# A pool of half-size weight tiles and more steps of weight preparation in the retention part of a hybrid RG-LRU, retention and conv-FFN block

## The chip, the core and the metric

The kernel runs on one NeuronCore of a Trainium2 chip. The engines named below are PE (TensorE, the matmuls), DVE (VectorE), ACT (ScalarE), POOL (GpSimd) and SP (SyncE, which issues the loads). The metric is the device time of one execution in microseconds (us); the time of the kernel before is the median of three runs.

## The reference

One layer over 512 tokens and 16 meta tokens (528 rows), model width 1024. Cut to what is computed:

```python
xn = rms_norm(h, norm_mix_g);  z = xn @ w_in                 # 1024 -> 10752
u_rnn, u_gate, q, k, v, g_ret, ga, gb = split(z)
o_a = rg_lru(causal_dwconv(u_rnn, ...), ...) * gelu(u_gate)  # width 1280
q, k = rotary(q), rotary(k) * RET_DK ** -0.5                 # 4 heads of 256
o = retention(q, k, v)                                       # decay-weighted, v is 4 heads of 512
o_b = head_rms(o) * silu(g_ret)
mixed = sigmoid(ga) * (o_a @ w_branch_rnn) + sigmoid(gb) * (o_b @ w_branch_ret)
h = h + mixed @ w_out
up = causal_dwconv(rms_norm(h, norm_ffn_g) @ w_up, ...);  gate, val = split(up)
h = h + (gelu(gate) * val) @ w_down
out = rms_norm(h, norm_final_g)[:, 16:]
```

## The kernel before, in words

Every float32 matrix is turned into a pair of float16 tiles, hi and lo, and each product is made of three float16 matmuls (hi·hi, hi·lo, lo·hi). A weight comes in units, listed in `units` in the order of use. `unit_load` fetches one unit (mostly 1 MB) into one of three `raw` buffers (pool `wraw`), SP's loads following one another. Its preparation is a list of steps in the queue `steps`. A step splits a part of the raw unit: ACT writes the hi half into a tile `wt` (L95), DVE the lo half (L96). A split of 1024 columns takes 1.05 us on ACT and 1.22 us on DVE, one of 512 columns 0.63 and 0.69.

A *plain* unit has two steps and fills two `wt` tiles. A *fast* unit is used in a scheme of seven products in place of eight (Strassen-like, 2 x 2 blocks). Its five steps in `fast_steps` are: B11 (a half-size form, 512 columns), then B21 and B22 together, then three sums in place on DVE (L263, L264, L265, 1.22 + 0.69 + 0.69 us), then T1 with T3, then T4 with T2. Its four forms lie in four `wt` tiles, the first of which is half empty. Pool `wsp` has ten such tiles.

What sets the order of the work: the program is emitted in the order of the code, while the tile framework orders each engine's queue by data and buffer dependences and by priority; within an engine instructions run in the order of its queue. Preparation is mixed in by `tick(n)`, which emits the next n steps, unless the units from the one in use (`current[0]`) to the step's own count more tiles than `ahead[0]` by `unit_tiles`: 4 for a fast unit, 2 for a plain one. `get(u)` emits whatever of unit u is still missing. `advance(run, ...)` takes a gate unit one product further and gives out one step. `keep` is ACT's copy of a finished product out of the PSUM bank `pa` (L928 in gates, L1022 in values), which the next product in `pa` waits for.

The stages that the change touches, with their times in the profiled execution: `values(0)` (to 250), `fast_values(1)` with scores of heads 2 and 3 (254 to 281), `retention_out(0)` and the gate of head 0 with the retention outputs of head 1 (`gated(0)`, 281 to 316), `fast_values(2)` (316 to 337), `gated(1)` (to 364), `fast_values(3)` (364 to 386), `gated(2)` (to about 413), the first mixing gates `gate_a` with the last head's gate (to about 497), and the second gates `gate_b` with their products (to 640). Then come the output projection, the up stage (to 935) and the down stage.

In a gate, DVE makes `g0` and `g1` from products and kept copies (L945, L949, L956), ACT applies the function (L961), and DVE multiplies into the retention output `or` (L1111). `head_norm` (L1087 to L1104) ends in two transposes of `rt` on DVE. `L1249` is the first part of the mixing.

## Time and profile before

| | |
|---|---|
| runs | 1054.64, 1054.85, 1055.18 us (median 1054.85) |
| the profiled execution's own time | 1054.74 us |
| its span, first to last instruction | 1053.0 us |
| mean granted TensorE clock | 0.998 |
| busy PE, DVE, ACT, POOL | 1036.3, 881.2, 590.9, 6.9 us |
| bytes moved by DMA | 111.52 MB, 106 GB/s in the mean |
| loads of `w_in`, 1 MB each | 34, landing 5.1 us after issue |
| PE idle from 220 to 639 us | 7.1 us in all |
| PE idle in the last 118 us | 6.9 us, nearly all after the last matmul |

How to read it: the profile is one execution, so times in rows are measured from its first instruction, 1.7 us of the execution's own time lying outside. Rows of the timeline give start, length, engine, line, operation and tile; the bracket at their end is the idle time of that engine just before, and the engine and line whose end released it. Matmuls overlap: a row of several is the time from the first's start to the last's end.

### The profile page before, as it was taken

Reading aid. Unit: us, or ns where it says so; the run is one execution under the profiler, and the core shown is the slowest. Engines: PE = TensorE matmul, PEld = TensorE weight load, DVE = VectorE, ACT = ScalarE, POOL = GpSimd, SP = SyncE. Lnnn points to the kernel's source line nnn. Section 1 sums busy time; section 2 is a strip of 40 time slices with the busy share of each in tenths; the row PEclk is TensorE's granted clock in tenths of the full one; section 3 lists DMA queues with packets and bytes.
Section 4 is the critical chain, followed back from the end, with each engine's and each line's share of the span. In section 5 each row is a group of like instructions: output and inputs, shape, how many; then the busy total and the mean of one; then the engine's idle time right before and its main releaser. Section 6 shows DMA issues by size and latency. Waiting matters only on the chain.

```text
span 1053.0 us, 21647 instructions
## 1 busy us (share of the span) xinstructions
PE 1036.3 (98%) x9283; PEld 873.9 (83%) x9283; DVE 881.2 (84%) x1332; ACT 590.9 (56%) x947; POOL 6.9 (1%) x20
## 2 busy tenths in 40 slices
PE   8999999999999999999999999999999999999997
PEld 6888888866888888888888885588888888888884
DVE  6997899898779999988797785489989888988965
ACT  8668934334566758766454453384555555454432
POOL 2000000000000000000000000000000000000000
PEclk9999999999999999999999999999999999999999
DMA  9241353221113123334333365032432324124312
GB/s 296 93 132 60 121 174 127 82 82 41 41 41 121 53 95 106 96 112 135 106 106 120 121 203 178 18 104 93 149 119 82 121 85 152 47 67 134 102 40 80
DMA packets 109343, 111.52 MB, mean 106 GB/s; under 512 B 5706, under 2 KB 101168, under 8 KB 109248
## 3 DMA queue, kind: packets, MB, share of 16 engines
q1 hardware_dynamic: 108672, 109.74, 32.7%
q8 instruction: 72, 1.18, 0.5%
q10 hardware_dynamic: 288, 0.27, 0.1%
q0 software_dynamic: 288, 0.14, 0.1%
q14 instruction: 23, 0.19, 0.1%
HBM read 108.04 MB, written 2.10 MB: 105 GB/s over the span
## 4 chain that ended last, share of the span: by engine, by line
PE 84%; DVE 10%; ACT 3%; issue 1%; DMA 0%; ACTq 0%; DVEq 0%
PE ps L435 36%; PE P L1637 10%; PE pa L922 9%; PE pe L922 4%; PE ps L1354 4%; PE pm L435 3%; DVE wt L96 3%; PE ps L449 3%; PE pb L922 2%; PE pa L1012 2%; PE pa L1524 2%; PE ps L1079 2%; PE pe L1012 1%; ACT wt L95 1%; DVE raw L263 1%
## 5 line engine op out<-in xcount | busy, mean ns | idle before, releaser
L435 PEld LDWEIGHTS <-wt 128*128 128x128 f16 x3840 | 372.8, 97 | 51.4
L96 DVE SCALAR_TENSOR_TENSOR wt<-raw,wt 128x1024 f16<-128x1024 f32 (+2 forms) x290 | 314.5, 1100 | 55.1 <-ACT wt L95 53.8
L95 ACT ACTIVATE wt<-raw 128x1024 f16<-128x1024 f32 (+2 forms) x290 | 271.2, 956 | 128.5 <-PE P L1637 23.1
L922 PEld LDWEIGHTS <-wt 128*128 128x128 f16 x2016 | 195.3, 97 | 32.4 <-issue 5.7
L435 PE MATMUL ps<-x2h,wt 128*128 128x258 f16 (+1 forms) x1184 | 196.2, 272 | 0.0
L435 PE MATMUL ps<-xh,wt 128*128 128x258 f16 (+4 forms) x1056 | 177.0, 274 | 0.0
L435 PE MATMUL ps<-x2l,wt 128*128 128x256 f16 (+1 forms) x592 | 160.9, 272 | 0.0
L435 PE MATMUL ps<-xl,wt 128*128 128x256 f16 (+4 forms) x528 | 140.6, 274 | 0.0
L1637 PE MATMUL P<-wt,act 128*128 128x256 f16 x792 | 88.3, 273 | 0.0
L1637 PEld LDWEIGHTS <-act 128*128 128x128 f16 x792 | 77.5, 98 | 9.0
L922 PE MATMUL pa<-xs,wt 128*128 128x258 f16 x576 | 71.3, 273 | 2.0 <-ACT kept L928 1.5
L1502 DVE SCALAR_TENSOR_TENSOR cv<-ps,vt,cv 128x512 f32<-128x512 f32 x80 | 59.5, 747 | 9.1 <-ACT cv L1500 8.5
L263 DVE TENSOR_TENSOR raw<-raw 128x1024 f32<-128x1024 f32 x45 | 54.9, 1221 | 0.7
L435 PE MATMUL pm<-oa,wt 128*128 128x256 f16 (+1 forms) x480 | 54.1, 273 | 0.0
L922 PE MATMUL pa<-ob,wt 128*128 128x257 f16 x384 | 45.7, 274 | 0.6 <-ACT last L928 0.5
L1354 PE MATMUL ps<-wt,mx 128*128 128x512 f16 x192 | 44.3, 378 | 0.0
L1500 ACT ACTIVATE cv<-ps,vt,vt 128x512 f32<-128x512 f32 x40 | 30.6, 766 | 11.9 <-PE ps L435 11.9
L1524 PEld LDWEIGHTS <-wt 128*128 128x128 f16 x336 | 32.6, 97 | 4.4
L1354 PEld LDWEIGHTS <-mx 128*128 128x128 f16 x192 | 17.6, 98 | 18.5
L1012 PEld LDWEIGHTS <-xs 128*128 128x128 f16 x288 | 27.8, 98 | 5.9 <-issue 2.8
L449 PEld LDWEIGHTS <-wt 128*128 128x128 f16 x288 | 27.9, 97 | 5.0 <-issue 0.6
L1079 PE MATMUL ps<-sc,v 128*128 128x257 f16 (+4 forms) x384 | 31.6, 236 | 0.0
(328 smaller groups left out, 1493.7 us busy)
## 6 DMA issues: line engine op xcount, KB each, us to landing
raw<-in_w_in SPq DMA_DIRECT2D x34, 1024.0 KB, 5.1
raw<-in_w_up SPq DMA_DIRECT2D x24, 1024.0 KB, 5.3
raw<-in_w_down SPq DMA_DIRECT2D x48, 256.0 KB, 3.8
raw<-in_w_in SPq DMA_DIRECT2D x16, 512.0 KB, 4.8
raw<-in_w_branch_ret SPq DMA_DIRECT2D x16, 512.0 KB, 4.5
raw<-in_w_branch_rnn SPq DMA_DIRECT2D x8, 640.0 KB, 4.9
raw<-in_w_out SPq DMA_DIRECT2D x4, 1024.0 KB, 5.2
xin<-in_x SPq DMA_DIRECT2D x4, 512.0 KB, 5.8
```

The source lines that it names most:

```text
L95: a = nc.scalar.activation(hi, src, AF.Copy, scale=s)
L96: b = nc.vector.scalar_tensor_tensor(lo, src, s, hi, op0=ALU.mult, op1=ALU.subtract)
L263: nc.vector.tensor_tensor(pair, pair, rv[:, :, right].rearrange("p (h k) c -> p h k c", h=2), op=ALU.add)
L435: nc.tensor.matmul(half_of(ps, halves, hf), w(aw, k, col, P), src(ax, k, c0, n), start=k == 0 and (aw, ax) == (0, 0), stop=k == nk - 1 and ...
L449: mm = nc.tensor.matmul(half_of(ps, halves, hf), w(aw, k, col, P), src(ax, k, c0, n), start=k == 0 and (aw, ax) == (0, 0), stop=k == KD - ...
L922: nc.tensor.matmul(ps[:, :n], ws[k // 4](wf, aw, k % 4), src(xf_, ax, k), start=first and k == 0 and (aw, ax) == (0, 0), stop=k == last_k ...
L1012: nc.tensor.matmul(ps[:, TH * tt:TH * tt + TH], x_form(xf_, ax, 2 * a + k, tt * P, P), ws[a](wf, aw, k), start=first and (a, tt, k, ax, aw ...
L1079: nc.tensor.matmul(ps[:, hf, s0 - lo_i:257], vd, st[SCP[b][0]][:, sa, o:o + hi_i - s0], start=i == 0, stop=i == len(todo) - 1)
L1354: nc.tensor.matmul(ps[:, n], mx[k][:, a, c0:c0 + P], wo[k // 2](aw, k % 2, n * 512, 512), start=k == 0 and (a, aw) == (0, 0), stop=k == ks ...
L1502: nc.vector.scalar_tensor_tensor(vv_, taps[j], vt2[:, 48 * j + ch:48 * j + ch + 1], vv_, op0=ALU.mult, op1=ALU.add)
L1524: nc.tensor.matmul(ps[:, :258], w(wf, aw, k), x2_form(xf_, ax, k), start=first and k == 0 and (aw, ax) == (0, 0), stop=k == 3 and aw == 1, ...
L1637: nc.tensor.matmul(pd[:, 256 * tt:256 * tt + 256], t[:, ax, c0 + tt * P:c0 + tt * P + P], w(wf, aw, i), start=q % 6 == 0 and tt == 0 and i ...
```

## The change

It does four things. (1) Pool `wsp` goes from 10 to 9 tiles, and a new pool `wsb` of 3 tiles of half the size (name `wb`) takes form B11 of the fast units. (2) `unit_tiles` counts 3 for a fast unit, and `ahead[0]` is 9 from `fast_values(1)` on; the changes to 12 and 10 in the values and second gates go. Since `gate_b` left 10 behind it, the output projection and the first part of the up stage now also run with 9 in place of 10. (3) In `retention_out(0)` every output gives out one step, with `current[0]` set to head 0's first gate unit; in `gated`, each retention output of the next head gives out one more. (4) `gate_b` no longer switches `ahead[0]`.

```diff
--- before.py
+++ after.py
@@ -60,7 +60,8 @@
     xp = ctx.enter_context(tc.tile_pool(name="xp", bufs=4))
     pieces = ctx.enter_context(tc.tile_pool(name="pieces", bufs=46))
     wraw = ctx.enter_context(tc.tile_pool(name="wraw", bufs=3))
-    wsp = ctx.enter_context(tc.tile_pool(name="wsp", bufs=10))
+    wsp = ctx.enter_context(tc.tile_pool(name="wsp", bufs=9))
+    wsb = ctx.enter_context(tc.tile_pool(name="wsb", bufs=3))
     work = ctx.enter_context(tc.tile_pool(name="work", bufs=8))
     small = ctx.enter_context(tc.tile_pool(name="small", bufs=4))
     psum = {}
@@ -250,9 +251,9 @@
 
         def cut(rows, cols):
             def run():
-                t = wsp.tile([P, 2, 1024], F16, name="wt")
                 src = rv[:, rows, cols]
                 n = bk * src.shape[2]
+                t = wsb.tile([P, 2, 512], F16, name="wb") if n == 512 else wsp.tile([P, 2, 1024], F16, name="wt")
                 tv = [t[:, a, :n].rearrange("p (k c) -> p k c", k=bk) for a in range(2)]
                 tiles.append(tv)
                 split(tv[0], tv[1], src, SW)
@@ -294,7 +295,7 @@
     current = [0]
 
     def unit_tiles(u):
-        return 4 if units[u][3] else 2
+        return 3 if units[u][3] else 2
 
     def emit_step():
         u, run = steps[done[0]]
@@ -1176,9 +1177,11 @@
                 head_norm(h)
             advance(a, "P7", "P6")
             next(other)
+            tick()
             scale_head(h, i)
             advance(a, "P2", "P5")
             next(other)
+            tick()
             for _ in a:
                 pass
         for _ in other:
@@ -1190,16 +1193,14 @@
     split_forms(1)
     rest(scores(1))
     psum_layout(acc=2, bank=4)
-    ahead[0] = 12
+    ahead[0] = 9
     fast_values(1, chain(scores(2), scores(3)))
-    ahead[0] = 9
+    current[0] = u_gr[0][0]
     for _ in retention_out(0):
-        pass
+        tick()
     gated(0)
     for h in range(2, 4):
-        ahead[0] = 12
         fast_values(h)
-        ahead[0] = 9
         gated(h - 1)
     gating[0] = False
 
@@ -1278,16 +1279,13 @@
 
     def gate_b(i):
 
-        ahead[0] = 10
         run = mix_unit(u_gb, i)
         advance(run, "P1", "P7", "P6")
-        ahead[0] = 12
         advance(run, "P2", "P5")
         rest(run)
         for _ in mix_products(i):
             tick(2)
         tick()
-        ahead[0] = 10
 
     gate_b(0)
     gate_a(3)
```

Instructions and bytes are the same in number. Line numbers of the new kernel are one higher from the pool on (L96 is L97 there). PE's order differs mainly in `fast_values(2)` and `fast_values(3)`: before, the framework had pulled the products of these stages into one another (some of `pb`'s matmuls between `pa`'s), and now each product's 24 matmuls stand together in the order of the code.

The first place is DVE's queue from head 0's gate to head 2's values. Before, the rows at the start of `fast_values(2)` are these; `raw_3792` is the second of its two units, its first row here (128x512) is B11, and `kept_4186` belongs to the values themselves:

```order
L1111 TENSOR_TENSOR or0_3634<-g1_3947,or0_3634 128x514
L956 TENSOR_TENSOR g0_3946<-pe_3962,kept_3944 128x257
L96 SCALAR_TENSOR_TENSOR wt_4137<-raw_3792,wt_4137 128x512
L96 SCALAR_TENSOR_TENSOR wt_4140<-raw_3792,wt_4140 128x1024
L1111 TENSOR_TENSOR or0_3633<-g0_3946,or0_3633 128x514
L263 TENSOR_TENSOR raw_3792<-raw_3792 128x2x2x256
L264 TENSOR_TENSOR raw_3792<-raw_3792 128x2x256
L1032 TENSOR_TENSOR kept_4186<-pb_4154,kept_4186 128x512
L265 TENSOR_TENSOR raw_3792<-raw_3792 128x2x256
L96 SCALAR_TENSOR_TENSOR wt_4146<-raw_3792,wt_4146 128x1024
```

In the new order the same unit is `raw_3666`. Its B11 and first sum stand much earlier, behind the last sum of `retention_out(0)` (`ssum_3638`) and ahead of the transpose of head 0's `head_norm`:

```order
L1088 TENSOR_TENSOR ssum_3638<-ssum_3638,sq_3698 128x514
L1088 TENSOR_TENSOR ssum_3638<-ssum_3638,sq_3730 128x514
L1088 TENSOR_TENSOR ssum_3638<-ssum_3638,sq_3762 128x514
L97 SCALAR_TENSOR_TENSOR wb_4045<-raw_3666,wb_4045 128x512
L264 TENSOR_TENSOR raw_3666<-raw_3666 128x2x2x256
L1101 STREAM_TRANSPOSE tr_3791<-rt_3789 128x512
```

B11 and L263 (now L264) of that unit moved from the values of head 2 to the gate of head 0, past some 35 rows of DVE.

The second place is ACT's queue from the end of head 0's second gate unit into the values of head 2. Before (`wt_4146` and `wt_4149` are the T forms of the second unit, `kept_4186` the first copy in the values):

```order
L961 ACTIVATE g1_3947<-pa_3948 128x257
L95 ACTIVATE wt_4137<-raw_3792 128x512
L95 ACTIVATE wt_4140<-raw_3792 128x1024
L961 ACTIVATE g0_3946<-g0_3946 128x514
L1022 ACTIVATE kept_4186<-pa_4152 128x512
L95 ACTIVATE wt_4146<-raw_3792 128x1024
L95 ACTIVATE v2_4216<-kept_4186 128x512
L95 ACTIVATE wt_4149<-raw_3792 128x1024
```

Now (the T forms are `wt_4119` and `wt_4152`; `or1` is the retention output, `g1` and `g0` the gate):

```order
L96 ACTIVATE ob_4084<-or0_3635 128x514
L96 ACTIVATE wt_4119<-raw_3666 128x1024
L1084 ACTIVATE or1_3829<-ps_4090 128x514
L1086 ACTIVATE sq_4116<-ps_4090 128x514
L962 ACTIVATE g1_3964<-g1_3964 128x257
L96 ACTIVATE wt_4152<-raw_3666 128x1024
L962 ACTIVATE g1_3964<-pa_3965 128x257
L96 ACTIVATE wt_4215<-raw_3858 128x1024
L962 ACTIVATE g0_3963<-g0_3963 128x514
L1023 ACTIVATE kept_4189<-pa_4155 128x512
```

The T forms of the second unit moved from behind the first copy of the values to ahead of `g1`, and the forms of the next gate unit (`raw_3858`) follow.

The third place is DVE's queue in the first mixing gate, up to the L956 of `g0` (here `g0_5470`). Before, from the add of `g1` (L949) on:

```order
L949 TENSOR_TENSOR g1_5471<-pe_5486,last_5469 128x257
L1129 TENSOR_TENSOR y_5546<-d_5545,or2_4477 128x257
L96 SCALAR_TENSOR_TENSOR ob11_5565<-or2_4476,ob11_5565 128x257
L96 SCALAR_TENSOR_TENSOR ob_5568<-or2_4477,ob_5568 128x514
L263 TENSOR_TENSOR raw_5308<-raw_5308 128x2x4x128
L264 TENSOR_TENSOR raw_5308<-raw_5308 128x4x128
L265 TENSOR_TENSOR raw_5308<-raw_5308 128x4x128
L96 SCALAR_TENSOR_TENSOR wt_5673<-raw_5308,wt_5673 128x1024
L96 SCALAR_TENSOR_TENSOR wt_5676<-raw_5308,wt_5676 128x1024
L96 SCALAR_TENSOR_TENSOR wt_5729<-raw_5504,wt_5729 128x640
L96 SCALAR_TENSOR_TENSOR wt_5751<-raw_5504,wt_5751 128x640
L96 SCALAR_TENSOR_TENSOR wt_5817<-raw_5632,wt_5817 128x512
```

Now (L957, of `g0_5481`):

```order
L950 TENSOR_TENSOR g1_5482<-pe_5497,last_5480 128x257
L97 SCALAR_TENSOR_TENSOR ob11_5579<-or2_4479,ob11_5579 128x257
L97 SCALAR_TENSOR_TENSOR ob_5582<-or2_4480,ob_5582 128x514
L97 SCALAR_TENSOR_TENSOR wt_5649<-raw_5250,wt_5649 128x1024
L97 SCALAR_TENSOR_TENSOR wt_5654<-raw_5412,wt_5654 128x640
L97 SCALAR_TENSOR_TENSOR wb_5759<-raw_5515,wb_5759 128x512
L97 SCALAR_TENSOR_TENSOR wt_5735<-raw_5412,wt_5735 128x640
L264 TENSOR_TENSOR raw_5515<-raw_5515 128x2x4x128
L97 SCALAR_TENSOR_TENSOR wt_5823<-raw_5515,wt_5823 128x1024
L97 SCALAR_TENSOR_TENSOR wt_5852<-raw_5515,wt_5852 128x1024
L265 TENSOR_TENSOR raw_5515<-raw_5515 128x4x128
L957 TENSOR_TENSOR g0_5481<-pe_5497,kept_5479 128x257
```

Before, one more form (`wt_5820`) and then L956 of `g0_5470` follow. Now the last difference and the last sum of the gate unit (`raw_5250`) stand ahead of `g1`'s add (L950), and `wb_5759` with the sums and two forms of a further unit (`raw_5515`) stand ahead of L957.

The fourth place is ACT's queue in the second gates, around the copy `last` of the first mixing product. Before and now:

```order
L928 ACTIVATE kept_6715<-pa_6719 128x257
L95 ACTIVATE wt_6809<-raw_6599 128x1024
L928 ACTIVATE kept_6715<-pa_6719 128x257
L95 ACTIVATE wt_6958<-raw_6698 128x640
L928 ACTIVATE last_6716<-pa_6719 128x257
L95 ACTIVATE wt_6974<-raw_6698 128x640
L95 ACTIVATE wt_6994<-raw_6745 128x512
```

```order
L962 ACTIVATE g0_6586<-g0_6586 128x514
L96 ACTIVATE wt_6812<-raw_6602 128x1024
L929 ACTIVATE kept_6718<-pa_6722 128x257 x2
L96 ACTIVATE wb_7137<-raw_6958 128x512
L96 ACTIVATE wt_6961<-raw_6701 128x640
L929 ACTIVATE last_6719<-pa_6722 128x257
L96 ACTIVATE wt_6977<-raw_6701 128x640
```

B11 of a unit two further on (`wb_7137` of `raw_6958`) stands ahead of `last`; before, that unit's rows came after the plain unit's and the `mx` forms.

## The prediction

> **What bounds the kernel now.** I read the busy shares and the chain of the page first, then PE's waits, then a table of stretches, then the timelines of the stalls.
>
> ```profile
> PE 1036.3 (98%) x9283; PEld 873.9 (83%) x9283; DVE 881.2 (84%) x1332; ACT 590.9 (56%) x947; POOL 6.9 (1%) x20
> ...
> PE 84%; DVE 10%; ACT 3%; issue 1%; DMA 0%; ACTq 0%; DVEq 0%
> ```
>
> PE is the bound: 98% busy and 84% of the chain. The change neither adds nor removes an instruction or a byte (one form of each fast unit goes to a smaller buffer), so PE's work stays and only its waits can move. PE's waits (summed us, times, longest) that the moved work can touch:
>
> ```profile
> PE pa L922 <- ACT kept L928: 1.5, 2, 1.0
> ...
> PE pe L922 <- DVE g L949: 1.0, 1, 1.0
> PE pa L1012 <- DVE wt L96: 0.9, 2, 0.5
> ...
> PE pa L1012 <- ACT wt L95: 0.6, 2, 0.4
> PE pa L1012 <- DVE sf L886: 0.6, 1, 0.6
> ...
> PE pa L1012 <- ACT kept L1022: 0.4, 2, 0.2
> ```
>
> Together 5.0 us, a little more by PE's pace (below): that caps the gain. By stretch (sum of PE, PEld, DVE, ACT busy in each):
>
> ```profile
> 282.00:312.00 30.00, 29.78 (x316) 26.37 (x315) 22.62 (x37) 18.08 (x32) 0.00 (x0) 1.00 0.16 51
> 312.00:337.00 25.00, 23.95 (x249) 20.37 (x247) 22.73 (x31) 17.17 (x26) 0.00 (x0) 1.00 0.29 87
> 337.00:361.00 24.00, 24.00 (x241) 21.26 (x239) 23.77 (x41) 16.11 (x29) 0.00 (x0) 1.00 0.26 87
> 361.00:386.00 25.00, 24.06 (x247) 20.49 (x245) 23.07 (x29) 16.82 (x25) 0.00 (x0) 1.00 0.29 92
> 386.00:410.00 24.00, 23.94 (x240) 21.06 (x238) 23.08 (x40) 16.64 (x29) 0.00 (x0) 1.00 0.21 65
> 410.00:448.00 38.00, 35.98 (x326) 31.47 (x325) 37.90 (x64) 28.98 (x48) 0.00 (x0) 1.00 0.38 115
> ...
> 750.00:935.00 185.00, 185.00 (x1688) 163.58 (x1687) 161.01 (x239) 101.54 (x155) 0.00 (x0) 1.00 0.32 102
> ```
>
> PE stands idle 1.05 us in 312 to 337 (the values of head 2), 0.94 in 361 to 386 (head 3), 2.02 in 410 to 448 (the first gates). DVE is nearly full from 312 to 448, idle only 2.27 + 0.23 + 1.93 + 0.92 + 0.10 = 5.45 us, but it has 7.38 us free in 282 to 312, just ahead. In the up stage (750 to 935) PE never stops.
>
> **The two stages of fast values.** First PE at head 2, then at head 3, then the two rows of DVE and ACT that it waits for:
>
> ```profile
> 318.83 0.27 PE L1012 MATMUL pa<-wt,xh 128*128 128x256 f16 x1 [0.47 <-DVE wt L96]
> ...
> 323.08 1.25 PE L1012 MATMUL pe<-wt,xs 128*128 128x256 f16 x10
> 324.72 0.27 PE L1012 MATMUL pa<-wt,xs 128*128 128x256 f16 x1 [0.38 <-ACT wt L95]
> ...
> 328.61 1.58 PE L1012 MATMUL pa<-wt,xs 128*128 128x256 f16 x13 [0.20 <-ACT kept L1022]
> ```
>
> ```profile
> 367.16 0.27 PE L1012 MATMUL pa<-wt,xh 128*128 128x256 f16 x1 [0.47 <-DVE wt L96]
> ...
> 373.05 0.27 PE L1012 MATMUL pa<-wt,xs 128*128 128x256 f16 x1 [0.27 <-ACT wt L95]
> ...
> 376.94 2.23 PE L1012 MATMUL pa<-wt,xs 128*128 128x256 f16 x19 [0.20 <-ACT kept L1022]
> ```
>
> ```profile
> 318.10 1.82 DVE L96 SCALAR_TENSOR_TENSOR wt<-raw,wt 128x512 f16<-128x512 f32 x2
> ```
>
> ```profile
> 321.68 1.06 ACT L95 ACTIVATE wt<-raw 128x1024 f16<-128x1024 f32 x1 [0.80 <-DVE raw L263]
> ```
>
> The brackets add up to the idle time of their stretches (0.47 + 0.38 + 0.20 = 1.05; 0.47 + 0.27 + 0.20 = 0.94). Each hides a little more: a matmul is shown for 0.27, yet in the row of ten the next starts (1.25 - 0.27)/9 = 0.11 later, so a stall costs its bracket plus 0.16. Head 2 costs 1.05 + 0.48 = 1.5 us, head 3 0.94 + 0.48 = 1.4.
>
> The cause is the second of the two value units. Its half-size form B11 is split on DVE only at 318.10, when PE already stands before it, and its T form reaches ACT at 321.68 because it waits for the sum in L263. Three whole fast units (nine whole tiles, three half ones) now fit, where ten tiles held two and a half. With the third unit allowed ahead, and a step given out by each retention output, the order has that B11 and that sum ahead of head 0's first L1101 transpose, and the last T forms ahead of `g1` and of L957 on head 0's second gate unit. What pays for them on DVE are the gaps there:
>
> ```profile
> 292.55 0.71 DVE L1100 STREAM_TRANSPOSE tr<-rt 128x512 f32<-128x512 f32 x1 [2.01 <-ACT rt L1096]
> ...
> 302.60 0.70 DVE L1087 TENSOR_TENSOR ssum<-ssum,sq 128x514 f32<-128x514 f32 x1 [1.48 <-ACT sq L1085]
> ```
>
> ```profile
> L96 DVE SCALAR_TENSOR_TENSOR wt<-raw,wt 128x1024 f16<-128x1024 f32 x221 | 268.4, 1220 | 41.0 <-ACT wt L95 40.0 <-DMA raw<-in_w_down 0.3
> ...
> L263 DVE TENSOR_TENSOR raw<-raw 128x1024 f32<-128x1024 f32 x45 | 54.9, 1221 | 0.7
> ```
>
> The gap before the transpose is 2.01 us. B11's split (1.82 - 1.22 = about 0.6 to 0.7 of the row at 318.10) and one sum (1.22) make 1.9: they fit. Counting every row of the two orders with its length in this trace, the moves put 8.8 us more DVE work ahead of head 0's second L956 than now. 7.4 us was free in 282 to 312, and part of the 2.27 of the next stretch. So that L956 comes less than 1 us later than now; the products that need its bank come more than that later, so I cost it at nothing. If the gaps are not filled, the 8.8 us lie on DVE ahead of the gate's adds, and PE waits in the gate instead. Bounds: 0 if the same waits come back, 2.9 if all six go. I take 2.7, nearer the upper end, because four of six waits are for the very rows that move: B11 moves up by 20 us of DVE work, the T forms by 1.3 us of work and by the filled gaps. The two for `kept` I count half, as they hang on ACT's order.
>
> **The first gates (410 to 448).**
>
> ```profile
> 430.88 1.48 PE L922 MATMUL pe<-xs,wt 128*128 128x258 f16 x12
> 433.34 1.48 PE L922 MATMUL pa<-xs,wt 128*128 128x258 f16 x12 [0.98 <-ACT kept L928]
> ...
> 447.72 0.27 PE L922 MATMUL pe<-xh,wt 128*128 128x258 f16 x1 [1.04 <-DVE g L949]
> ```
>
> ```profile
> 422.18 0.42 DVE L949 TENSOR_TENSOR g<-pe,last 128x257 f32<-128x257 f32 x1
> ...
> 431.93 0.42 DVE L956 TENSOR_TENSOR g<-pe,kept 128x257 f32<-128x257 f32 x1
> ```
>
> ```profile
> 432.92 0.37 ACT L928 ACTIVATE kept<-pa 128x257 f32<-128x257 f32 x1
> ```
>
> PE left `pa`, the source of `kept`, before 430.88, but ACT first has `g0` to do, which waits for L956 at 431.93. Between L949 and L956 stand 9.75 us of DVE work. In the new order this stretch has the same kinds of rows, the last of the four differences (0.42) and one half sum (0.69) fewer, which now stand ahead of L950: about 1.0 us shorter, so the stall of 0.98 + 0.16 shrinks to about 0.1. From L956 to the L949 that PE waits for at 447.72 the amount of DVE work is the same in both orders, DVE being full, so the second stall does not shrink by itself: it may even keep all of its 1.2. Bounds: a gain of both (2.3) down to a loss of 3.1, since 3.1 us more form work stands ahead of L956 than now, counted from the start of the program; without the idle time spent earlier it would come that much later. I take a gain of 1.0, by the row count of the stretch itself.
>
> **The rest.** The stall before head 1's values (0.6, on `sf` of L886) follows values(0); three early B11 splits and sums now lie in the rotary stage, ahead of it. Bounds 0 and 0.76; I take 0.3. In the up and down stages plain units go from five ahead to four; 24 units in 185 us are 7.7 us each, so four are 31 us of cover against some 5.3 us of load and 5 us of splits: nothing, and had that cover gone, a load would show in the 750 row. In the second gates (497 to 640) the half forms now come earlier in ACT's order, and they wait for loads:
>
> ```profile
> 517.65 1.06 ACT L95 ACTIVATE wt<-raw 128x1024 f16<-128x1024 f32 x1 [2.41 <-DVE raw L265]
> ...
> 524.82 0.39 ACT L928 ACTIVATE last<-pa 128x257 f32<-128x257 f32 x1 [0.59 <-PE pa L922]
> ```
>
> ```profile
> 519.99 7.82 SPq L107 DMA_DIRECT2D raw<-in_w_branch_ret  x4
> ```
>
> ```profile
> raw<-in_w_branch_ret SPq DMA_DIRECT2D x16, 512.0 KB, 4.5
> ```
>
> ACT's row at 517.65 is the last reader but one of a raw buffer; the unit that takes this buffer is issued at 519.99 and lands some 4.5 us later, at 524.5. Its B11 is now ahead of `last` at 524.82, with one 0.74 split between. If the load still lands at 524.5, `last` starts about 524.5 + 0.63 + 0.7 = 525.8, and PE waits 1.0 us more. But the row at 517.65 also moves ahead of the `kept` before it, and its sum comes earlier on DVE, so the load can be issued some 2 us sooner, which covers the 1.0. Bounds for the whole stage: a gain of 1.4 (the other `kept` wait there, 0.5 + 0.16, and its like) and a loss of 12 units x 1.0. I take a loss of 0.2: a unit's load mostly comes sooner with its form, and a few places have less than 1 us of margin.
>
> **Sum.** -2.7 - 1.0 - 0.3 + 0.2 = -3.8 us on the profiled execution (span 1053.0, its own time 1054.74): 1050.9. The median of the runs is 0.1 above that execution, so 1051.0.
>
> **Rivals.** (1) The waits only move. PE would reach the first gates 2.7 us sooner, where DVE is busy 37.90 of 38 us; if DVE has not got ahead by then, both stalls there grow by what was won. For it: DVE's 5.45 us of idle time from 312 to 448 is little. Against it: the 7.4 us before 312 are filled. That leaves the 0.3, 1054.4 or so; within the 0.2% (2.1 us) that a measurement of this kernel can tell from no change. That the change does nothing (the extra step finds no buffer or no landed load, so the order's moves bring no earlier start) ends in the same place, 1054.8.
>
> (2) Slower: a half form waits for its load in front of `last` or `kept`, in the second gates. Place: ACT, as at 524.82. Price 1.0 us in each of 12 fast units if no load is issued sooner, against 4.0 won: 1054.85 + 8.0 = 1062.9 at the worst. It decides from 0.33 us a unit (4.0/12) upward; at 0.6 it gives 1058.0. For it: ACT starts each instruction behind the one before it, as 432.92 shows, where `kept` waits behind `g0`. Against: ACT is idle 44% of the span and the load has room to move. [...]
>
> (3) More: both stalls of the first gates go, and the `kept` waits of the second gates: 2.9 + 2.3 + 0.7 + 0.6 = 6.5, so 1048.3.
>
> **How the numbers follow.** The forecast has 0.52 (1049.8 to 1052.6 as its own range), rival (3) 0.14, rival (1) with "no effect" 0.23, rival (2) 0.11. Faster by over 0.2% is forecast plus (3), 0.66; same 0.23; slower 0.11. The range leaves out the far half of (3) and all of (2): 1048.8 to 1054.9.
>
> **What would show it.** Right: no wait of L1013 for `wt` in the stages of heads 2 and 3, PE idle in each under 0.3 us, DVE's gaps from 287 to 303 filled, one stall near 430 gone and the one 14 us behind it still there at 0.5 to 1.2. Wrong: waits of `pa` or `pe` for `kept`, `last` or `g` that are new between 285 and 320 or 497 and 640, and ACT rows of half forms that wait for a raw load's landing.

## The result, and the profile after

The changed kernel takes 1056.9 us in the median of 12 runs (1056.04 to 1057.95), against 1054.84 for the kernel before (1054.64 to 1055.21): 1.0021 times as long, 95% interval 1.0012 to 1.003. The forecast was 1051.0, so it missed by 5.9 us and on the wrong side. Of the runs below, one execution of e2_noticks took 3848 us; its comparison leaves that one out.

The profiled execution spans 1055.1 us, 2.1 more than before. The shares and the chain of its page:

```profile
PE 1035.5 (98%) x9283; PEld 874.0 (83%) x9283; DVE 879.6 (83%) x1332; ACT 589.2 (56%) x947; POOL 6.9 (1%) x20
...
PE 78%; DVE 15%; ACT 4%; DMA 1%; issue 1%; ACTq 0%; DVEq 0%
```

The work is the same; the chain that ended last runs through DVE more often (15%, before 10%). PE's waits (us in total, times, longest):

```profile
PE pa L923 <- ACT kept L929: 5.2, 6, 1.9
PE pa L923 <- ACT last L929: 1.8, 2, 1.3
...
PE pa L1013 <- DVE wt L97: 1.0, 1, 1.0
PE pe L923 <- DVE g L950: 1.0, 1, 1.0
```

The waits for `kept` grew from 1.5 to 5.2 us; the waits of the value stages for forms are down to one. By stretch (busy PE, PEld, DVE, ACT, as before):

```profile
282.00:312.00 30.00, 29.78 (x317) 26.47 (x315) 27.33 (x42) 21.08 (x37) 0.00 (x0) 1.00 0.16 51
312.00:337.00 25.00, 25.00 (x258) 22.01 (x257) 19.75 (x29) 13.09 (x22) 0.00 (x0) 1.00 0.33 110
337.00:361.00 24.00, 23.10 (x238) 20.51 (x237) 23.93 (x39) 19.80 (x34) 0.00 (x0) 1.00 0.14 45
361.00:386.00 25.00, 24.02 (x244) 20.93 (x243) 22.00 (x30) 13.12 (x21) 0.00 (x0) 1.00 0.36 112
386.00:410.00 24.00, 22.70 (x236) 20.26 (x235) 22.22 (x37) 19.04 (x32) 0.00 (x0) 1.00 0.14 45
410.00:448.00 38.00, 34.79 (x310) 30.29 (x308) 36.41 (x62) 25.67 (x43) 0.00 (x0) 1.00 0.39 118
```

DVE's idle time ahead of 312 is filled as the forecast said (7.38 to 2.67 us), and PE no longer stops in 312 to 337 (1.05 to 0.00). But DVE then stands 5.25 us in that stretch (2.27 before), and PE loses in every later one but 361 to 386, where it stays: 0.90, 1.30 and 3.21 us for 0.00, 0.06 and 2.02.

A ledger shows where the lead went. PE runs 9283 matmuls in both kernels, so the start of the matmul with the same number can be compared; at these places both kernels have the same matmul under that number (but for e21 at 589.0). Each entry is worked out from two traces: that start in the named kernel minus that in the kernel before (minus: ahead). The head of a column is the time in the kernel before: ends of the values of heads 1, 2 and 3, then four places in the gates and the first mixing gates, the start of the second gates, and two places in them, the last at their end.

```
                 275.5 332.3 380.6 413.0 430.7 446.4 466.1 509.2 589.0 633.5
changed kernel   -0.62 -2.59 -2.26 -1.05 -0.05 +0.92 +1.05 +2.23 +1.39 +2.02
e1_pool          -0.68 -0.73 -0.24 -0.24 -0.12 -0.14 -0.70 +2.30 +1.46 +2.09
e2_noticks       -0.76 -1.08 -0.54 -0.54 -0.32 -0.35 -1.11 +3.77 +2.93 +3.56
e3_ticks         -0.05 +0.20 +0.32 +0.57 +0.55 +0.10 +0.03 +0.03 +0.03 +0.03
e5_two           -0.89 -1.91 -1.57 -1.77 -0.08 -0.34 +1.22 +2.13 +1.29 +1.92
e6_half2         -1.07 -1.95 +0.40 +3.35 +3.32 +2.20 +3.26 +10.2 +10.3 +10.9
e7_ten           +5.91 +3.92 +4.51 +5.91 +6.91 +8.69 +9.24 +10.7 +9.79 +10.7
e9_nine          -1.01 -0.18 +0.87 +1.92 +1.93 +2.68 +2.16 +4.64 +4.02 +4.62
e11_inorder      -0.34 -2.31 -1.83 -1.92 -1.36 -1.54 -0.53 +1.69 +1.49 +2.03
e13_inpool       -0.47 -0.26 -0.06 -0.06 -0.07 -0.07 +0.39 +3.49 +3.30 +3.85
e19_hold         -0.78 -2.76 -3.05 -1.88 -1.90 +2.03 +0.77 +1.48 +0.64 +1.31
e20_bhold        -0.16 -0.42 -0.68 -0.68 -0.68 -0.47 -0.61 -0.61 -1.33 -1.33
e21_inhold       -0.50 -2.47 -2.19 -1.78 -1.81 -1.39 -0.78 +2.77 +1.97 +3.89
e22_hold_all     -0.72 -2.69 -1.50 +0.03 +0.01 -1.13 -1.91 -1.91 -0.25 +2.34
e24_hold_gates   -0.92 -2.90 -1.70 -0.18 -0.20 -1.34 -2.12 +0.30 -0.28 +0.39
e25_bhold_gates  -0.15 -0.50 +0.32 +0.85 +0.82 -0.32 +0.17 +2.36 +1.63 +1.63
```

The changed kernel is 2.26 us ahead at 380.6, where the forecast's terms so far make 3.0. It then loses 3.18 us up to 446.4 and 1.31 from there to 509.2. Two of the places, each as PE, ACT and DVE see it. At 351 (the gate of head 1):

```profile
352.39 0.82 PE L923 MATMUL pa<-xs,wt 128*128 128x258 f16 x6 [0.90 <-ACT kept L929]
```

```profile
351.43 0.63 ACT L962 ACTIVATE g<-g 128x514 f32<-128x514 f32 x1 [1.79 <-DVE g L957]
351.97 0.37 ACT L929 ACTIVATE kept<-pa 128x257 f32<-128x257 f32 x1
```

```profile
349.17 0.69 DVE L1168 TENSOR_TENSOR or<-or,rt 128x514 f32<-128x514 f32 x1
...
350.98 0.42 DVE L957 TENSOR_TENSOR g<-pe,kept 128x257 f32<-128x257 f32 x1
```

`kept`, which only copies a finished product, stands behind the activation of the previous unit's `g0`, and that waits 1.79 us for the add L957, which DVE reaches at 350.98 behind a run of rows without a gap. ACT does nothing else in that time. In the kernel before, the same copy stands in front of `g0`; ACT and DVE there:

```profile
353.57 0.39 ACT L928 ACTIVATE kept<-pa 128x257 f32<-128x257 f32 x1
353.84 0.65 ACT L961 ACTIVATE g<-g 128x514 f32<-128x514 f32 x1
```

```profile
352.30 0.42 DVE L956 TENSOR_TENSOR g<-pe,kept 128x257 f32<-128x257 f32 x1
```

DVE reaches the add 1.32 us sooner in the changed kernel, but PE is 2.59 us ahead, and with `g0` in front of `kept` it has to wait for DVE. At 414 the two have changed places in the same way. At 432 `g0` stood in front in the kernel before as well, and now a half form stands in between too:

```profile
434.25 0.93 PE L923 MATMUL pa<-xs,wt 128*128 128x258 f16 x7 [1.95 <-ACT kept L929]
```

```profile
431.47 0.63 ACT L962 ACTIVATE g<-g 128x514 f32<-128x514 f32 x1 [1.96 <-DVE g L957]
433.30 0.63 ACT L96 ACTIVATE wb<-raw 128x512 f16<-128x512 f32 x1 [1.20 <-DMA raw<-in_w_in]
433.83 0.37 ACT L929 ACTIVATE kept<-pa 128x257 f32<-128x257 f32 x1
```

The stalls at 414 (1.0 us, behind `g0`) and 467 (0.9, behind a T form and `g0`) have this pattern as well; at 408 (1.4) it is `last` that stands behind splits held up by a half form that waited 2.8 us for its load. At 432 the last matmul into `pa` starts at 429.84 and takes 0.27 us, but `kept`, which copies it, starts only at 433.83, behind two rows of ACT that wait 1.96 us for DVE and 1.20 us for a load.

### The profile page after: what moved, and what is told of

Same layout as the page of the kernel before. It is cut to its first block, busy times and chain, and to the rows that moved or that the text cites. A ratio compares the mean times of both kernels' runs of the same rounds, so it can differ in the third digit from the quotient of the medians.

```text
span 1055.1 us, 21619 instructions
## 1 busy us (share of the span) xinstructions
PE 1035.5 (98%) x9283; PEld 874.0 (83%) x9283; DVE 879.6 (83%) x1332; ACT 589.2 (56%) x947; POOL 6.9 (1%) x20
## 4 chain that ended last, share of the span: by engine, by line
PE 78%; DVE 15%; ACT 4%; DMA 1%; issue 1%; ACTq 0%; DVEq 0%
PE ps L436 36%; PE P L1635 10%; PE pa L923 7%; DVE wt L97 4%; PE ps L1352 4%; PE pe L923 3%; PE ps L450 3%; PE pa L1013 2%; PE pa L1522 2%; PE pb L923 2%; PE pm L436 2%; ACT wt L96 1%; PE ps L1080 1%; DVE ob L97 1%; DMA raw<-in_w_in 1%; PE pe L1522 1%
## 5 line engine op out<-in xcount | busy, mean ns | idle before, releaser
L436 PEld LDWEIGHTS <-wt 128*128 128x128 f16 x3840 | 372.8, 97 | 51.5
L97 DVE SCALAR_TENSOR_TENSOR wt<-raw,wt 128x1024 f16<-128x1024 f32 (+2 forms) x245 | 286.5, 1178 | 44.1 <-ACT wt L96 43.4
L96 ACT ACTIVATE wt<-raw 128x1024 f16<-128x1024 f32 (+2 forms) x245 | 245.2, 1019 | 104.8 <-DVE raw L266 34.8
L923 PEld LDWEIGHTS <-wt 128*128 128x128 f16 x1728 | 167.5, 97 | 33.6 <-issue 11.4
L264 DVE TENSOR_TENSOR raw<-raw 128x1024 f32<-128x1024 f32 x45 | 55.1, 1224 | 2.0 <-DMA raw<-in_w_down 0.8
L97 DVE SCALAR_TENSOR_TENSOR wb<-raw,wb 128x512 f16<-128x512 f32 x45 | 30.8, 689 | 18.0 <-ACT wb L96 18.0
L96 ACT ACTIVATE wb<-raw 128x512 f16<-128x512 f32 x45 | 27.8, 623 | 30.2 <-DMA raw<-in_w_in 12.7
L923 PE MATMUL pa<-ob,wt 128*128 128x257 f16 x288 | 33.8, 274 | 0.7 <-ACT last L929 0.5
L450 PEld LDWEIGHTS <-wt 128*128 128x128 f16 x288 | 27.9, 97 | 5.0 <-issue 0.6
```

What stands on the lines that cost most here:

```text
L96: a = nc.scalar.activation(hi, src, AF.Copy, scale=s)
L97: b = nc.vector.scalar_tensor_tensor(lo, src, s, hi, op0=ALU.mult, op1=ALU.subtract)
L264: nc.vector.tensor_tensor(pair, pair, rv[:, :, right].rearrange("p (h k) c -> p h k c", h=2), op=ALU.add)
L436: nc.tensor.matmul(half_of(ps, halves, hf), w(aw, k, col, P), src(ax, k, c0, n), start=k == 0 and (aw, ax) == (0, 0), stop=k == nk - 1 and ...
L450: mm = nc.tensor.matmul(half_of(ps, halves, hf), w(aw, k, col, P), src(ax, k, c0, n), start=k == 0 and (aw, ax) == (0, 0), stop=k == KD - ...
L923: nc.tensor.matmul(ps[:, :n], ws[k // 4](wf, aw, k % 4), src(xf_, ax, k), start=first and k == 0 and (aw, ax) == (0, 0), stop=k == last_k ...
```

## The experiments

### Which part of the change costs

The pools alone in the kernel before; the changed kernel without its added steps (three `tick` lines and the line of `current[0]` out); the steps alone in the kernel before.

```diff
# e1_pool (on the kernel before)
+    wsb = ctx.enter_context(tc.tile_pool(name="wsb", bufs=3))   # wsp: bufs 10 -> 9
+    t = wsb.tile(...) if n == 512 else wsp.tile(...)
# e2_noticks (on the changed kernel); e3_ticks: the same lines into the kernel before
-    current[0] = u_gr[0][0]
     for _ in retention_out(0):
-        tick()
+        pass
```

> Only the pools of the change (nine whole tiles, three half ones); fast units still count 4, the limits of 12, 9 and 10 and the places of the steps are those of before. Theory L (loads): the loss comes from the third unit in the gates, whose half form ACT meets while its load is still in flight, with a keep behind it; here the gates stay at two units, so no new wait, and only the values of heads 2 and 3 can gain: 1053.3 to 1054.8. Theory D (DVE): the loss comes from the additional steps, which put forms ahead of the gate's adds on a full DVE; none are added here, so the same 1053.3 to 1054.8. The run says what the pools alone are worth.

> The change without the additional steps in retention_out(0) and in the gates of the heads; pools, count of 3 and limit of 9 stay. Theory L: the third unit is still asked for in the gates, so waits of ACT for loads stay at 5 us or more in all and the time stays at 1056 to 1057.5. Theory D: with the steps gone the gate's adds come as before: 1054.8 or less, and the waits of PE for kept at 351 and 414 are gone.

> Kernel before with only the additional steps in retention_out(0) and in the gates of the heads; ten whole tiles, count of 4, limits of before. Theory L: two units in the gates, so ACT's half forms meet no flying load there: 1052.5 to 1054.8. Theory D: the steps alone bring the loss: 1056 to 1057.5, with kept waits at 351 and 414.

Measured: e1 1056.97 us (1.0024, interval 1.0015 to 1.0033); e2 1058.31 (1.0029, 1.0018 to 1.0039); e3 1054.79 (1.0, 0.9991 to 1.0009). The pools alone cost as much in all as the whole change, the steps alone nothing. Theories L and D both had e1 at 1053.3 to 1054.8 and both missed; D, that the steps bring the loss, missed e2 and e3 as well. e2 lies 1.4 us above the changed kernel, but that the steps save time on top of the pools is not shown: the two intervals overlap, and of e2's seven executions three took 1057.02 to 1057.22 us at a mean granted clock of 0.998 and four 1058.25 to 1059.13 at 0.996 or 0.997 (see the last section).

By place the steps do matter, and equal totals hide it. From 380.6 to 446.4 the changed kernel loses 3.18 us and e2 only 0.19: without the steps PE is only 0.54 us ahead there, the stall at 414 is gone, and the bracket of the one at 351 falls from 0.90 to 0.36. Instead e2 loses 4.1 us from 446.4 to 509.2. In e1 nearly all of the loss goes in one place, between 466 and 509 (-0.70 to +2.30). ACT there, first in the kernel before, then in e1:

```profile
464.29 1.06 ACT L95 ACTIVATE wt<-raw 128x1024 f16<-128x1024 f32 x1 [1.41 <-DVE raw L263]
465.25 0.37 ACT L928 ACTIVATE kept<-pa 128x257 f32<-128x257 f32 x1
467.62 0.63 ACT L961 ACTIVATE g<-g 128x514 f32<-128x514 f32 x1 [2.00 <-DVE g L956]
```

```profile
466.39 1.06 ACT L96 ACTIVATE wt<-raw 128x1024 f16<-128x1024 f32 x1 [2.21 <-DVE raw L266]
467.36 0.62 ACT L962 ACTIVATE g<-g 128x514 f32<-128x514 f32 x1
467.88 0.37 ACT L929 ACTIVATE kept<-pa 128x257 f32<-128x257 f32 x1
```

The same copy comes 2.63 us later. In both kernels a form that waits for a sum stands in front of it; in e1 that sum is the last of its three (L266) and no longer the first, and `g0` stands in front too. Probably the shortage of tiles had kept that form back before; no run shows this by itself.

### Fewer units ahead, other pool sizes

e5 lets two units ahead instead of three in the gates; e6 gives two half tiles; e7 ten whole and three half (paid with two `pieces`); e9 is the kernel before with nine whole tiles and no half ones.

```diff
# e5_two            # e6_half2, e7_ten, e9_nine: bufs of
+    ahead[0] = 6   #   wsb 3 -> 2;  wsp 9 -> 10 and pieces 46 -> 44;  wsp 10 -> 9
```

> The change with the limit at two fast units (6) in all gates and mixing products, and three (9) in the values and from the output projection on. Theory L: the waits of ACT's half forms for loads go back under 2 us in all and the time falls to 1052 to 1054; the wait at 318 stays gone or small. Theory D: the added steps are still there, but they are stopped by the limit; some of the forms still come early: 1055 to 1057.

> The change with two half tiles in place of three; nine whole tiles stay. The pools alone cost 2.1 us and the steps alone nothing, so the cause lies in the pools. Theory Q (queue): a half form that has a free tile of its own is put early into ACT's queue and stands there for its load, with keep and other forms behind it; with two half tiles the third unit's half form has to wait for a tile again, ACT's waits for loads of w_in in half forms fall from 12.7 to under 4 us, and the time is 1053.5 to 1055.2. Theory S (supply): nine whole tiles are one too few, and the forms behind the half form wait for a tile; these stay nine, so 1056 to 1058.

> The change with the tenth whole tile back beside the three half tiles (room for it from the pool of pieces, 44 in place of 46, which moves a few rows after 460 us). Theory Q: the half forms still find free tiles and ACT still stands at loads, 10 us or more in all: 1056 to 1058. Theory S: the tenth tile lets the later forms in: 1051.5 to 1054.5, and the waits of PE for wt at 369 us are gone.

> Kernel before with nine whole tiles in place of ten and no half tiles; nothing else. Theory Q: no half form gets ahead of its load, so it stays within 1 us of before, 1054.3 to 1055.8. Theory S: the lost tile costs at least what the pools of the change cost, 1056.5 to 1059.

Measured: e5 1057.31 (1.0024), e6 1065.13 (1.0099), e7 1064.96 (1.0096), e9 1059.53 (1.0052, 1.0039 to 1.0064). Theory L, the third unit, fell with e5, and so did its premise: ACT's waits of half forms for loads of `in_w_in` rose from 12.7 to 15.3 us there. e6 and e7 lie far outside the numbers of both theories; what two half tiles in place of three do is not followed here beyond one wait (last section). Theory Q gives no reason for the loss of e9, which has no half tiles, and theory S put it 0.5 us too low. Against the kernel before on the same chip, one whole tile less costs 4.9 us (e9), and the half pool gives 2.7 of it back (e1, 2.1). e7 is spoiled as a test of theory S: 5.9 of its 10.7 us are lost before the values of head 1, mostly in one wait of 4.7 us that neither kernel has. Even so it loses 4.8 after that, where the changed kernel loses 2.6. No gain of the tenth tile shows, but the run also takes two `pieces` away, and it cannot tell the one from the other.

### Half forms off ACT

e10 makes the hi part of the half forms on POOL, so that ACT never waits for their loads.

```diff
+    nc.gpsimd.tensor_scalar_mul(tv[0], src, SW)      # half forms only
```

> The change with the hi half of every half form made on POOL (GpSimd, idle 99% of the span) in place of ACT; the lo half stays on DVE. Theory Q: ACT no longer stands at loads (0 us in half forms), the waits of PE for last at 407 and kept at 432 shrink by 1 us or more each; what DVE then waits for may eat part: 1053.5 to 1056. Theory S: tiles as in the change, so 1056 to 1058 as now.

Measured: 1070.83 us (1.015, 1.0136 to 1.0163). The groups of e10 and of the changed kernel:

```profile
L260 POOL TENSOR_SCALAR wb<-raw 128x512 f16<-128x512 f32 x45 | 91.4, 2033 | 915.1 <-DMA raw<-in_w_in 315.9
```

```profile
L96 ACT ACTIVATE wb<-raw 128x512 f16<-128x512 f32 x45 | 27.8, 623 | 30.2 <-DMA raw<-in_w_in 12.7
```

POOL needs 2.03 us for what takes ACT 0.62, and DVE waited 38.6 us in all for it. Theory Q, that ACT stands at loads, was neither borne out nor refuted by this; the next runs take these waits away in another manner.

### Half forms in order

In the changed kernel 35 of the 45 half forms pass forms of older units on ACT. Here a half form is issued behind the split before it: e11 in the changed kernel, e13, e14, e15 in e1, e5, e2.

```diff
+    with tc.issue_after(last_form[0]) if n == 512 else nullcontext():
         a, _ = split(tv[0], tv[1], src, SW)
+    last_form[0] = a
```

> The change, with each half form issued behind the split emitted just before it, so that it can't overtake: in ACT's order of the change 35 of 45 half forms stand ahead of 107 forms of older units, before none, here none. Theory O (overtaking): the half tile of its own lets the half form (and the sum behind it) of a younger unit pass the older units' forms, which wait for whole tiles; it meets a flying load and takes DVE's time from more urgent forms. Then ACT's waits for loads in half forms fall from 12.7 us (w_in) to under 3 us, and the time is 1051 to 1054. Theory S2 (tiles): nine whole tiles delay the whole forms whatever the order: 1056 to 1058.

> The pools alone (1056.97) with the half forms held behind the split before them; limits, counts and steps of before. Theory O: 1053.5 to 1055, at or below the kernel before, since 45 half forms take no whole tile. Theory S2: 1056.5 to 1058.5, as the pools alone.

> The change with two units in the gates, three in the values (1057.31), and the half forms held behind the split before them. Theory O: 1052.5 to 1055. Theory S2: 1056.5 to 1058.5.

> The change without its additional steps (1058.31), and the half forms held behind the split before them. Theory O: 1052.5 to 1055; against the run with steps it says what the steps are worth once nothing overtakes, 0 to 1.5 us. Theory S2: 1057 to 1059.

Measured: e11 1056.7 (1.002, 1.0011 to 1.0028), e13 1058.64 (1.0037), e14 1058.2 (1.0039), e15 1058.7 (1.0038). ACT's waits of half forms for loads of `in_w_in` are gone in e11, and from 380.6 to 446.4 it loses only 0.3 us where the changed kernel loses 3.2. But the waits for `kept` are 5.7 us in 8, and 3.2 us go between 446.4 and 509.2. Theory O, that passing is the cause, holds in the first gates and fell as the whole cause. Theory Q fell with it: e13 has none of these waits either, and neither kernel is clearly faster than the same one with them. Theory S2, that nine whole tiles delay the whole forms in any order, has e11, e14 and e15 in its ranges and e13 0.1 us above; no run tests it by itself.

### `g0` behind the next unit's first copy

Theory K: the cause is the order on ACT's queue. e19 (in the changed kernel) and e20 (in the kernel before) move `g0`'s activation, and what it finishes, behind the first `kept` of the next unit; e22 issues all forms and sums behind the last `kept` as well, from the second stage to the end of the mixing.

```diff
         keep(kept[:, h0], pa, 0)
+        drain()                              # tails, issued after last_keep
...
-        func(g0[:, :TQ], g0[:, :TQ], 1.0, 0); finish(0, g0)
+        tails.append(tail)                   # tail(): these two calls
# e22 besides
-        return [cut(top, left), cut(low, ...), sums, late(...), late(...)]
+        return [held(cut(top, left)), held(cut(low, ...)), sums, late(...), late(...)]
# and issue_after(last_keep) holds until the end of the mixing
```

> The changed kernel with one thing moved: the activation of a unit's g0 and what finishes it (and the mix of an even chunk) are issued behind the first kept copy of the next unit instead of in front of it. Pools, planner limits and ticks stay as in the changed kernel. Theory K (the loss is kept copies that stand on ScalarE's in-order queue behind rows that wait for VectorE): the stalls at 351, 414, 432 and 467 (1.06, 1.03, 2.11 and 0.87 us) lose their g0 part, TensorE's waits for kept fall from 5.2 us to 2.5 or less, and the time is 1052 to 1054 us. Rival C (ScalarE and VectorE are simply late there, whatever stands in front): the waits for kept stay near 5 us or turn into waits for last and g, and the time stays at 1056 to 1058 us.

> The kernel before with the same move alone: g0's activation behind the next unit's first kept copy. Theory K: the kernel before has one such place, 1.14 us at 432, and loses about that: 1053.5 to 1054.2 us, waits for kept 0.5 to 1 us. Rival C: no change within 0.1 per cent, 1054.8 us, or slower, since what g0 feeds comes later.

> The changed kernel with the same move, and besides every split of a weight form and every sum that takes part in it issued behind the last kept copy, from the second stage on and through the mix, so that neither g0 nor a form stands in front of a kept copy that was written ahead of it. Theory K: waits for kept under 1.5 us and a time of 1051 to 1053.5 us. Rival C: the forms come later, TensorE waits for forms (wt, wb) instead, and the time is 1056 us or more.

Measured on one chip (kernel before 1054.64): e19 1056.74 (1.002, 1.0011 to 1.0028), e20 1053.47 (0.9989, 0.998 to 0.9998), e22 1056.7 (1.002, 1.0011 to 1.0029).

e19 lost the stalls at 351 and 414, as theory K said, and at 380.6 it is 3.05 us ahead. Then it loses 3.9 us in one place, and its time lies where rival C had put it. ACT and PE there:

```profile
432.39 0.63 ACT L96 ACTIVATE wb<-raw 128x512 f16<-128x512 f32 x1 [3.71 <-DMA raw<-in_w_in]
432.93 0.37 ACT L936 ACTIVATE kept<-pa 128x257 f32<-128x257 f32 x1
```

```profile
433.35 1.81 PE L930 MATMUL pa<-xs,wt 128*128 128x258 f16 x12 [2.90 <-ACT kept L936]
435.67 3.58 PE L436 MATMUL pm<-oa,wt 128*128 128x256 f16 x22 [0.51 <-DVE m L1262]
```

The half form that waits for its load now stands alone in front of `kept`. And after 2.90 us of standing still the same rows take longer (1.81 for 12 matmuls, 1.48 elsewhere; 3.58 for 22, 2.58 in e20).

e20 came out where theory K had put it, 1053.5, but barely clear of the noise and for other reasons than written: at 432 the wait for `kept` only became one for `m`, which is deferred with `g0`.

```profile
PE pm L435 <- DVE m L1261: 1.2, 1, 1.2
```

Its gain is 0.7 us up to 380.6 and 0.7 at 587, where ACT reaches `kept` two us sooner. ACT in the kernel before and in e20:

```profile
585.70 1.06 ACT L95 ACTIVATE wt<-raw 128x1024 f16<-128x1024 f32 x1 [2.72 <-DVE raw L263]
586.67 0.37 ACT L928 ACTIVATE kept<-pa 128x257 f32<-128x257 f32 x1
```

```profile
584.63 0.39 ACT L935 ACTIVATE kept<-pa 128x257 f32<-128x257 f32 x1 [0.24 <-PE pa L929]
```

e22 has no wait for `kept` left in its list, and is 1.91 us ahead of the kernel before at 509.2. Then the forms of the second gates come too late, and it loses 4.3 us (to +2.34), as rival C had said. Its largest waits from 509 to 640:

```profile
PE pe L937 <- DVE wt L97: 1.2, 4, 0.4
PE pe L937 <- DVE g L966: 1.0, 3, 0.4
```

### Holding only where it helped, and both orders mended

e24 is e22 with forms held only to the end of the first mixing gates; e25 is the same two edits in the kernel before; e21 is e19 and e11 together.

```diff
# e24_hold_gates (on e22); e25_bhold_gates: all of it on the kernel before
+    mixing[0] = False          # ends the holding of forms
     gate_b(0)
```

> The changed kernel, with weight forms and sums issued behind the last kept copy from the second stage to the end of the gates (up to 510 us) and no further, and the activation of g0 behind the next unit's first kept copy throughout. Theory K, now by stage: up to 510 us it keeps what holding everything showed (TensorE idle 4.8 us between 220 and 510, against 8.9 in the changed kernel and 5.7 in the kernel before), and from 510 on it loses what the changed kernel loses (1.5 us between 510 and 639) and not the 3.5 us that holding the forms cost there: 8.9 - 4.8 = 4 us less than the changed kernel, so 1052.5 to 1053.5 us. Rival C (ScalarE and VectorE have no more room, the waits only move): 1055.5 us or more.

> The kernel before with the same two edits (forms held up to 510 us, g0 held throughout): the pools of before, so the forms of heads 2 and 3 still start late. Theory K: the half-tile pools are worth the removed waits in the value stages (about 1 us at 312 to 337) once the order is the same, so this lies 0.5 to 2 us above the changed kernel with the same edits, at 1053 to 1055 us. Rival C': the pools are worth nothing or less, and this is as fast as that one or faster.

> The changed kernel with both orders mended: a half form is issued behind the split before it (as in the in-order run), and the activation of g0 behind the next unit's first kept copy (as in the hold run). The hold run left one place worse: at 430 the kept copy stood behind a half form that waited 3.7 us for its load. Here neither stands in front. Theory K (the order on ScalarE's queue): the in-order run's stalls at 351, 413 and 431 (0.98, 0.59, 0.87 us) and half of that at 466 (0.96) go, about 2.9 us of its 1056.7: 1053.5 to 1054.5 us. The stalls at 451 and 505 (1.36, 1.26), which have weight forms and not g0 in front, stay. Rival C (the waits only move): 1055.5 us or more, with new waits for last, g or forms of about the same sum.

Measured: e24 1054.94 (1.0002, 0.9993 to 1.0011), e25 1056.45 (1.0017, 1.0008 to 1.0026), both on one chip, and no run of the one (1054.8 to 1055.21) reaches the other (1056.31 to 1056.75); e21 1058.7 (1.0038, 1.0025 to 1.0052).

With the same order rules the change (pools, limits and steps) saves 1.5 us (e24 against e25), as expected of the difference. Both times lie 1.4 us above the upper end of what was expected, and in the kernel before the two edits cost 1.8 us (e25). In e24 part of that is at the seam where the holding ends: three held forms that wait for a sum come out in front of `kept`. ACT in e24:

```profile
501.08 2.95 ACT L96 ACTIVATE wt<-raw 128x1024 f16<-128x1024 f32 x3 [3.74 <-DVE raw L266]
503.94 0.36 ACT L943 ACTIVATE kept<-pa 128x257 f32<-128x257 f32 x1
```

e21 refutes theory K as a recipe: the stalls at 351 and 413 are gone, but the one at 431 stays in two parts, those at 466 and 505 grow (from 1.0 to 1.5 and from 1.3 to 2.1 us), and new ones come at 377 and 591 (1.0 and 1.7). Rival C's words, that the waits only move, describe it:

```profile
PE pa L935 <- ACT kept L941: 4.5, 5, 1.9
PE pa L935 <- ACT last L941: 2.0, 2, 1.5
PE pe L935 <- DVE g L964: 2.0, 3, 1.2
```

What is shown: each large stall of the changed kernel that is followed to its place here is a copy that PE waits for, standing on ACT's queue behind a row that waits for DVE or a load. Moving that row removes the stall: those at 351 and 414 go in e19 and the one at 467 falls from 0.71 to 0.23 us (brackets), and the one at 408 goes in e11. The one at 432, with two such rows, is gone only where the forms are held too (e22, e24). This did not make the whole faster: e11, e19, e21 and e22 all take 1056.7 us or more, as other waits came.

What stays open: why nearly any change of the pools makes the sum of such waits larger. One stretch stands out. From 446.4 to 509.2 every kernel of the ledger with nine whole tiles loses 1.3 us or more except e19 and e22, and e3 and e20, with ten tiles, lose nothing; but e7 and e25 have ten too and lose 2.0 and 2.7, so the tenth tile alone does not decide it. The change gives +2.1 us in the order as it was, +3.3 with `g0` moved (e19 against e20), -1.5 with the forms held as well (e24 against e25); the half pool alone gives -2.7 beside nine whole tiles (e1 against e9). The sign hangs on the order around it, and no rule for it was found.

## Why the prediction was wrong, point by point

- **The bound and the cap.** PE stayed the bound and its work the same. That the waits of the kernel before cap the gain was not put to the test; no run is further ahead than 3.05 us (e19 at 380.6). Nothing capped the loss, and the sum had only one small term for one. Added up by place, the terms up to 380.6 brought 3.2 us for 3.0 forecast; 0.96 in the gate of head 1 and 1.31 after 446, which had no term, and 3.18 in the first gates, for which 1.0 of gain was taken, went the other way, and 0.2 came back in the second gates.
- **Head 1's `sf` stall** (0.3 taken): right. Its bracket fell from 0.60 to 0.20 us; the rest of the 0.62 by which PE is ahead at 275.5 was won before that stall.
- **Fast values** (2.7 taken: 1.5 in head 2, 1.4 in head 3, cut a little): head 2 gave 1.97 (from -0.62 to -2.59), 0.4 more than its three stalls cost, which is not followed further. Head 3 gave 0.63 (from -1.63 at 364 to -2.26): its three waits went, and one of 1.1 us came at 369, a T form that waits for the last sum. The mechanism and the sum (2.6) held, the sizes of the two parts did not.
- **"I cost it at nothing"**, said of head 0's second L956: this held. DVE reaches that add at 317.30 for 317.76 before, and PE does not stop there. The idle time ahead of 312 was filled, though 3 us of it came back as DVE idle time in 312 to 337 (5.25 against 2.27).
- **Head 1's gate** had no term, since PE did not stop there before. It cost 0.96 us between 332.3 and 364: the lead of PE met an add on DVE that had gained less, with `g0` now in front of `kept` on ACT. The text compared ACT's order at the gate of head 0 and in the second gates, but not here.
- **The first gates** (a gain of 1.0 taken): the step that failed most. From 380.6 to 446.4 PE loses 3.18 us. The text had worked out this very bound, "a loss of 3.1, since 3.1 us more form work stands ahead of L956", and set it aside for a count of the rows between two adds on DVE (whose 9.75 us include the first add; between them lie 9.33). The loss lies at 408 (1.21 up to 413.0), 414 (1.00) and 432 (0.97). The count of rows was no measure: DVE did reach L957 at 431.01, sooner than the 431.93 of before, and yet `kept` came at 433.83 for 432.92, as ACT had a half form and its load in front of it. What failed is the step from DVE's row count to the copy: the wait was to end with L956, and it ended behind other rows of ACT's queue. The second stall there stayed, as the text said (0.96 us, before 1.04). The range should have kept that bound; that the loss agrees with its 3.1 is luck, as it was worked out for a later L956.
- **From 446 to 509** no term was given; it cost 1.31 us. The order of `kept` against `g0` and the T forms on ACT, which decided it at 466, was never compared there.
- **The second gates** (a loss of 0.2 taken): a gain of 0.21 from 509.2 to 633.5. Rival (2) has its mechanism right, a half form waiting for its load in front of `kept` or `last`, but placed it here, where it did not bite; it came at 408 and 432. There it is one part beside `g0`.
- **Rival (1)** was nearest in its mechanism: what was won in the value stages was lost in the first gates, where DVE is nearly full, and more on top.

## What to carry to other kernels

Where an engine with room to spare serves the bound engine from an in-order queue, read that queue's order at each copy that the bound engine waits for: what stands in front of it after the change, and what that row waits for. More buffers let work come earlier, and a shortage may have been what kept it out of the way, so a buffer change must be priced by the copies that it can now overtake, and by a range that holds the same pattern's loss. A gain that is there at one place (2.3 us ahead at 380) says little about the end while the next stage's queues are full.

The kernel before with `g0` moved behind the next unit's first copy (e20, 1053.47 us) is faster than both, though only 0.1% faster than the kernel before, and its interval ends at 0.9998.

## What the runs showed of the hardware

A wait of PE cost more than itself in e2 (2.77 us), e19 (2.90) and e6 (3.34). After 1.95 us (432, changed kernel) the granted clock from 410 to 448 stays at 1.00. After 2.90 us (e19) the twelve matmuls behind it take 1.81 us for 1.48, as shown, and the granted clock from 410 to 448 is 0.96. In e6, after 3.34:

```profile
473.03 2.74 PE L923 MATMUL pa<-xs,wt 128*128 128x258 f16 x12 [3.34 <-ACT kept L929]
475.56 6.65 PE L436 MATMUL pm<-oa,wt 128*128 128x256 f16 x44
```

```profile
470.00:480.00 10.00, 6.97 (x38) 5.04 (x38) 4.27 (x7) 2.94 (x5) 0.00 (x0) 0.66 0.31 103
```

Twelve matmuls take 2.74 us for 1.48, and the granted clock of these ten us is 0.66. Of the waits followed here, the shortest with this effect and the longest without it lie close together. First e2, then e7:

```profile
468.09 1.68 PE L923 MATMUL pa<-xs,wt 128*128 128x258 f16 x12 [2.77 <-ACT kept L929]
469.30:472.60 3.30, 3.30 (x18) 2.33 (x16) 0.54 (x1) 0.39 (x1) 0.00 (x0) 0.50 0.91 294
```

```profile
442.02 1.48 PE L923 MATMUL pa<-xs,wt 128*128 128x258 f16 x12 [2.75 <-ACT kept L929]
442.00:452.00 10.00, 9.98 (x91) 8.86 (x91) 9.73 (x19) 8.40 (x12) 0.00 (x0) 1.00 0.02 5
```

In these two executions the granted clock is 0.50 from 469.3 to 472.6 after 2.77 us (e2), and 1.00 from 442 to 452 after 2.75 us (e7). No fixed limit is shown by this: e2's executions fall into two groups by time and granted clock, as given above, so by the author's estimate the same wait has the effect in some of them and not in others. Only one of them has a trace.
